# Hybrid decoder layer on one core: x transposed and w_in grouped by the host

## The chip, the cores and the metric

The kernel runs on one core of a Trainium2 chip. Its time is device microseconds of one execution, lower is better; several executions are timed and the median is given. Before the change the median of three is 529.26 us (526.42 to 530.28). One further execution was recorded by the hardware profiler; it took 522.21 us, and every row shown here comes from it.

The engines are TensorE (PE for matrix products, PEld for the loading of their stationary operand), VectorE (DVE), ScalarE (ACT), GpSimd (POOL) and SyncE (SP, which issues most transfers). Sixteen DMA engines move data between HBM and on-chip memory.

## What is computed

One decoder layer over 512 tokens of width 1024, in float32. Cut to what matters here:

```python
proj = x @ w_in                                   # (512,1024) @ (1024,2824)
ml_qk, ml_v, ml_o, ml_i, ml_f, a_q, a_k, a_v = jnp.split(proj, SPLIT_POINTS, axis=-1)
y = concat([mlstm_heads(...), sliding_window_attention(...)]) @ w_out
x = layer_norm(ALPHA * x + y)
x = layer_norm(ALPHA * x + hierarchical_moe(x))   # 32 experts, 4 groups, top 2 inside one group
```

The input projection is the first product of the layer. Everything else follows from it: the eight gate columns, the attention heads, the mLSTM heads, the output projection, the router, and at last 32 experts of 3 MB of weights each.

## The kernel before, in words

**The projection.** TensorE contracts over the partition axis, so x is needed with its 1024 features on partitions. The 512 tokens go in four chunks of 128 (`c` = 0 to 3). `xc[c]` receives a chunk as it lies in memory, tokens on partitions, 4 KB per token. `x_t(c)` transposes it with eight TensorE transposes of 128 by 128 into two PSUM banks, and then `split` writes each quarter (`q`, two blocks of 128 features) as a high part (`xh`, ScalarE, rounded to the fast float32 form) and a remainder (`xl`, VectorE, source minus high part).

**The weights.** `w_in` has 2824 columns and is taken in eleven groups of 264 or 256 columns, listed in `COLS`. `load_w(i)` fetches group `i` on SP's queue, the first group in three pieces (3, 3 and 2 blocks of 128 rows), the others in two pieces of four blocks. In memory a row of a group is one run of 1056 or 1024 bytes, and the next row is 11,296 bytes further on. `split_w(i)` splits each piece into `wh` and `wl` in the same way as x.

**The units.** `unit_att(i, c)` multiplies chunk `c` by one of the first three groups: 24 products, for each of the eight feature blocks high by high (line 244), low by high (line 245) and high by low (line 249). I call `unit_att(0, 0)` the first unit, `unit_att(0, 1)` the second, and so on; the fifth is `unit_att(1, 0)`. In the first unit all eight line-249 products come last, because the remainder `wl` is late. The next chunk's `x_t(c + 1)` is called inside a unit: before feature block 6 in the first unit, ahead of the second and third units otherwise. After these come the units for the mLSTM columns.

**The start.** SP issues in this order: `xc[0]`, the three pieces of group 0, `xc[1]` to `xc[3]`, then the pieces of group 1 and onward, as buffers come free. TensorE begins with `heat(WARM)`, products on zeros whose result nobody reads, then the transposes of chunk 0, then `heat(WARM2)`, then the first unit. The order on TensorE, VectorE and SP is the order of the code; ScalarE's is also in that opening part. GpSimd issues the small loads (biases, convolution weights, rotary tables) with its own queue, and later computes the rotary embedding (`rope`) for the attention heads, whose first input is the ScalarE copy `tq` of the fifth unit (line 271).

**After the projection.** Expert weights of the six static experts are fetched when the projection's loads are all issued; the others can only be fetched when the router has chosen the order. The x that the residual needs is loaded a second time, in its natural layout.

Of the kernel before, what the change touches and what calls it, by code (L numbers as in the profile page):

```python
# [22 lines left out]
DM = 1024  # L23
NCH = 4
P = 128
DIN = 2824
NE = 32
DE = 256
CAP = 64

ORDER = "BBBCABABABBCC"
NP = len(ORDER)
STATIC = 6
# [22 lines left out]
def place():  # L56

    na, nb = ORDER.count("A"), ORDER[STATIC // 2:].count("B")
    first = iter(range(STATIC))
    a, b = iter(range(STATIC, STATIC + na)), iter(range(STATIC + na, STATIC + na + 2 * nb))  # L60
    c = iter(range(STATIC + na + 2 * nb, NE))
    seats, base, cap = [], [0] * NE, [0] * NE
    for p, kind in enumerate(ORDER):
        src = {"A": (a, c), "B": (b, b), "C": (c, c, c, c)}[kind] if p >= STATIC // 2 else (first, first)
# [9 lines left out]
def ap_of(src, offset, dims):  # L74
    return bass.AP(tensor=src.tensor, offset=src.offset + offset, ap=dims)
# [1 line left out]

@with_exitstack
def layer_kernel(ctx, tc, x, w_in, conv_w, conv_b, gate_bias, norm_w, sinks, w_out, ln1_w, ln1_b,
                 w_gr, b_gr, w_er, b_er, w_gate, w_up, w_down, ln2_w, ln2_b, cos_t, sin_t, seat_t, out,  # L80
                 dbg=None):
    nc = tc.nc
    V, A, G, TE, SP = nc.vector, nc.scalar, nc.gpsimd, nc.tensor, nc.sync
# [36 lines left out]
    def bank(name, n=512, tag="m"):  # L120
        return PS.tile([P, n], F32, tag=tag, name=name, bufs={"m": 4, "t": 2, "pj": 2}[tag])
# [4 lines left out]

    x2 = x.rearrange("b s d -> (b s) d")
    o2 = out.rearrange("b s d -> (b s) d")
    win = w_in[0]
    xd = DR.tile([T, DM], F32, name="xd")  # L130

    yd = DR.tile([KEPT * P, DM], F32, name="yd")


    COLS = [(2048, 264), (2312, 256), (2568, 256)] + [(256 * i, 256) for i in range(8)]
    raws = {}

    THIRDS, HALVES = ((0, 3), (3, 3), (6, 2)), ((0, 4), (4, 4))
# [1 line left out]
    def wslot(name, i, m, dt=F32):  # L140
        t = slot(name, dt, "wr" if i else "ring0")
        return t[:, :m * COLS[i][1]].rearrange("p (j n) -> p j n", j=m)


    def wpair(i, m):
        if i:
            return [wslot(t, i, m, F32R) for t in ("wh", "wl")]
        n = m * COLS[0][1]
        t = slot("wh", F32R, "ring0")
        return [t[:, k * n:(k + 1) * n].rearrange("p (j n) -> p j n", j=m) for k in range(2)]  # L150

    def load_w(i):
        c0, n = COLS[i]
        raws[i] = []
        for j, m in THIRDS if i == 0 else HALVES:
            t = wslot("wraw", i, m)
            SP.dma_start(t, ap_of(win, j * P * DIN + c0, [[DIN, P], [P * DIN, m], [1, n]]))
            raws[i].append(t)

    xc = []  # L160
    for c in range(NCH):
        t = slot("xc")[:, :DM]
        SP.dma_start(t, x2[c * P:(c + 1) * P])
        xc.append(t)
        if c == 0:
            load_w(0)

    ident = C.tile([P, P], F32, name="ident")
# [19 lines left out]
    def split(hi, lo, src, eng=V):  # L188
        A.activation(hi, src, AF.Copy)  # L189
        eng.tensor_tensor(lo, src, hi, op=OP.subtract)  # L190
# [22 lines left out]
    xh = [slot("xh", F32R, "xt").rearrange("p (j n) -> p j n", j=2) for _ in range(4)]  # L213
    xl = [slot("xl", F32R, "xt").rearrange("p (j n) -> p j n", j=2) for _ in range(4)]

    def x_t(c):
        for g in range(2):
            p_ = bank("xt").rearrange("p (j n) -> p j n", j=4)
            for j in range(4):
                k = g * 4 + j  # L220
                TE.transpose(p_[:, j], xc[c][:, k * P:(k + 1) * P], ident)
            for h in range(2):
                q = g * 2 + h
                split(xh[q][:, :, c * P:(c + 1) * P], xl[q][:, :, c * P:(c + 1) * P],
                      p_[:, 2 * h:2 * h + 2])
                yield


    ws = {}
# [31 lines left out]
    def unit_att(i, c, late=False, mid=None):  # L261
        n = COLS[i][1]
        off = [0, 264, 520][i]
# [392 lines left out]
    with tc.manual_schedule(engines={ENG.PE, ENG.DVE, ENG.Activation}):  # L656
        warm = W.tile([P, P], F32, name="trif", bufs=1)
        V.memset(warm, 0.0)
        p_ = bank("warm")
# [449 lines left out]
    def pass_gu(xs, b, p, mid=None, parts=()):  # L1109
        pg = bank("pg")  # L1110
        for i in range(4):
            if i == 3 and mid:
                mid()
            if i and len(parts) >= i:
                parts[i - 1]()
            gu_part(pg, xs, b, pairs[p], TILES[ORDER[p]], i)
        return pg
# [25 lines left out]
    def pass_dn(ht, p):  # L1143
        return dn_mm(ht, pairs[p], TILES[ORDER[p]])

# [48 lines left out]
    q = C.tile([P, 5, 8], F32, name="slq")  # L1194
# [195 lines left out]
    with tc.manual_schedule(engines=MAN):  # L1390
# [108 lines left out]
        pgs = [bank("pg")]  # L1499
        gu_part(pgs[0], xs, 0, pairs[0], TILES[ORDER[0]], 0)  # L1500
        px = slots_b1()
# [11 lines left out]
    with tc.manual_schedule(engines={ENG.PE}):  # L1513
# [3 lines left out]
        h = pair_h(pgs[0])  # L1517
# [3 lines left out]
        h = pair_h(pgs[1])  # L1521
# [71 lines left out]
    with tc.manual_schedule(engines={ENG.PE, ENG.DVE}):  # L1593
        for p in range(2, NP - 1):
# [6 lines left out]
            h = pair_h(pg)  # L1601
# [66 lines left out]
    p = NP - 1  # L1668
    release(p - 1, True)
    prefetch(99)  # L1670
    with tc.manual_schedule(engines=MAN):
# [41 lines left out]
        h = pair_h(pg)  # L1713
# [44 lines left out]
    with tc.For_i(0, nmore, 1):  # L1758
# [20 lines left out]
_INS = ["x", "w_in", "conv_w", "conv_b", "mlstm_gate_bias", "mlstm_norm_w", "attn_sinks", "w_out",  # L1779
        "ln1_w", "ln1_b", "w_group_router", "b_group_router", "w_expert_router", "b_expert_router",  # L1780
        "w_exp_gate", "w_exp_up", "w_exp_down", "ln2_w", "ln2_b"]
# [8 lines left out]
            np.ascontiguousarray(np.concatenate([-s, s], 1)))  # L1790


def extra_inputs():
    _, base, cap = place()
    t = np.zeros((NE, 98), np.float32)
    t[:, 0:32], t[:, 32:64] = base, cap
    e = np.arange(NE)
    t[:, 96] = np.where(e < STATIC, 2000 * (STATIC - e), 0) + (NE - 1 - e) / 64
    t[:, 64:96] = t[:, 96]
    t[:, 97] = e  # L1800
    return list(zip(("rope_cos", "rope_sin", "seat_tab"), rope_tables() + (t,)))
# [19 lines left out]
```

## Time and profile before

| | us |
|---|---|
| median of three timed runs | 529.26 (526.42 to 530.28) |
| the profiled execution, whole | 522.21 |
| its span, first to last instruction | 520.5 |
| PE busy in the span | 475.8 (91%) |
| PEld, DVE, ACT, POOL busy | 324.1, 284.3, 161.2, 156.3 |
| line 221, the transposes of x, 32 products | 5.1 busy |

All positions in time are microseconds from the start of the span. A group of rows gives an engine's busy time, and the brackets at the end of a row say how long the engine stood idle before it and what ended that idle time. Adjacent instructions of one kind are merged into one row with a count. A product is pipelined, so the durations of neighbouring products overlap; the pace of a series is read from the starts. The profiled execution lies 7 us under the median of the timed runs.

### The profile page before, as it was taken

To read this page: it belongs to the slowest core of one execution; us is meant where nothing else is said; L and a number is where in the kernel's file an instruction comes from. 1 tells how busy PE (TensorE), PEld (TensorE's weight loads), DVE (VectorE), ACT (ScalarE), POOL (GpSimd) and SP (SyncE) were. 2 spreads that over 40 slices of the span, in tenths; PEclk is the share of its full clock that TensorE was granted. 3 is DMA by queue.
4 is the path that set the end of the run, shared out by engine and by line. 5 is a ranking of instruction groups with operands and counts; after the bars stand their busy time and mean duration, and the time that the engine had idled before them with its cause. 6 is when DMAs were issued, how large, how long until landed. Compare 5 with 4: busy or idle time off the path is not lost. (4 is left out here: it accounts for less than half of the span.)

```text
span 520.5 us, 8320 instructions
## 1 busy us (share of the span) xinstructions
PE 475.8 (91%) x2992; PEld 324.1 (62%) x2992; DVE 284.3 (55%) x635; ACT 161.2 (31%) x349; POOL 156.3 (30%) x178
## 2 busy tenths in 40 slices
PE   6999899999999999979799999999799949999881
PEld 6999678879899987758654736272263533353320
DVE  3543697984278685597876303012032036776953
ACT  3552565786444231333320202111021101131310
POOL 5579904323120100655650000000002334300431
PEclk9999999999999999999789999999899979998996
DMA  8724212220983548195929999999999999999740
GB/s 222 227 82 127 77 42 81 82 81 25 346 318 82 169 156 230 66 345 170 375 83 351 399 341 393 393 411 422 412 421 414 418 415 413 423 420 421 319 162 21
DMA packets 44605, 134.71 MB, mean 259 GB/s; under 512 B 6734, under 2 KB 18014, under 8 KB 41232
## 3 DMA queue, kind: packets, MB, share of 16 engines
q1 hardware_dynamic: 41504, 126.04, 64.7%
q0 software_dynamic: 3056, 8.10, 4.3%
q8 instruction: 24, 0.39, 0.3%
q14 instruction: 21, 0.17, 0.1%
HBM read 127.11 MB, written 8.91 MB: 261 GB/s over the span
## 5 line engine op out<-in xcount | busy, mean ns | idle before, releaser
L1106 PE MATMUL pg<-we,xs 128*32 128x512 f32 (+1 forms) x608 | 99.9, 601 | 3.3 <-DMA we<-in_w_exp_up 3.3
L1106 PEld LDWEIGHTS pg<-we,xs 128*32 128x32 f32 (+1 forms) x608 | 27.7, 120 | 60.6 <-issue 56.0
L244 PE MATMUL pj<-wh,xh 128*128 128x256 f32 (+1 forms) x224 | 63.3, 285 | 0.9 <-ACT wh L189 0.9
L245 PE MATMUL pj<-wh,xl 128*128 128x256 f32 (+1 forms) x224 | 62.3, 281 | 0.0
L1019 PE MATMUL xp<-ohr,x1h 128*128 128x256 f32 x192 | 51.3, 304 | 10.0 <-DVE xs L1025 8.2
L249 PE MATMUL pj<-wl,xh 128*128 128x256 f32 x192 | 52.5, 280 | 0.0
L1139 PE MATMUL yo<-we,ht 128*32 128x512 f32 (+1 forms) x304 | 50.0, 609 | 0.5 <-DVE ht L1131 0.5
L1019 PE MATMUL xp<-ohr,x1l 128*128 128x256 f32 x192 | 49.9, 297 | 0.0
L1019 PEld LDWEIGHTS xp<-ohr,x1h 128*128 128x128 f32 x192 | 39.4, 205 | 15.1 <-DVE xs L1025 8.4
L1157 POOL DMA_DIRECT2D yd<-y x8 | 4.4, 552 | 128.5 <-ACT y L1156 128.5
L244 PEld LDWEIGHTS pj<-wh,xh 128*128 128x128 f32 x224 | 42.1, 188 | 1.2 <-ACT wh L189 1.1
L245 PEld LDWEIGHTS pj<-wh,xl 128*128 128x128 f32 x224 | 42.1, 188 | 0.0
L1019 PEld LDWEIGHTS xp<-ohr,x1l 128*128 128x128 f32 x192 | 39.4, 205 | 0.0
L1131 DVE COPY ht<-ph 128x256 f32<-128x256 f32 x13 | 5.5, 423 | 57.1 <-PE ph L1129 57.1
L1121 ACT ACTIVATE hid<-pg 128x256 f32<-128x256 f32 x13 | 5.0, 383 | 101.8 <-PE pg L1106 101.8
L249 PEld LDWEIGHTS pj<-wl,xh 128*128 128x128 f32 x192 | 35.6, 188 | 0.0
L190 DVE TENSOR_TENSOR wl<-wraw,wh 128x1024 fp32r<-128x1024 f32 x14 | 21.5, 1552 | 22.7 <-ACT wh L189 14.4
L1139 PEld LDWEIGHTS yo<-we,ht 128*32 128x32 f32 (+1 forms) x304 | 14.2, 121 | 27.8 <-issue 25.8
L189 ACT ACTIVATE wh<-wraw 128x1024 fp32r<-128x1024 f32 (+2 forms) x23 | 23.2, 1021 | 11.8 <-PE pj L194 3.4
L193 PE MATMUL pj<-xh,wh 128*128 128x512 f32 x64 | 25.7, 402 | 0.0
L195 PE MATMUL pj<-xl,wh 128*128 128x512 f32 x64 | 25.5, 399 | 0.0
L1191 DVE TENSOR_TENSOR x<-x,cb 128x512 f32<-128x512 f32 x32 | 20.6, 680 | 9.0 <-PE cb L1190 8.9
(357 smaller groups left out, 964.3 us busy)
## 6 DMA issues: line engine op xcount, KB each, us to landing
we<-in_w_exp_gate SPq DMA_DIRECT2D x64, 512.0 KB, 12.4
we<-in_w_exp_up SPq DMA_DIRECT2D x64, 512.0 KB, 12.2
we<-in_w_exp_down SPq DMA_DIRECT2D x26, 1024.0 KB, 12.9
wraw<-in_w_in SPq DMA_DIRECT2D x20, 512.0 KB, 3.4
we<-in_w_exp_down SPq DMA_DIRECT2D x12, 512.0 KB, 10.3
yd<-y POOLq DMA_DIRECT2D x8, 512.0 KB, 7.9
xc<-in_x SPq DMA_DIRECT2D x4, 512.0 KB, 9.3
wo<-in_w_out SPq DMA_DIRECT2D x8, 256.0 KB, 4.3
```

Source lines behind the costliest of these rows:

```text
L189: A.activation(hi, src, AF.Copy)
L190: eng.tensor_tensor(lo, src, hi, op=OP.subtract)
L193: TE.matmul(o, lh, rh, start=start, stop=False)
L195: TE.matmul(o, lh, rl, start=False, stop=stop)
L244: TE.matmul(o, xh[j // 2][:, j % 2, cs], ws[i][j][0], start=j == 0, stop=False)
L245: TE.matmul(o, xl[j // 2][:, j % 2, cs], ws[i][j][0], start=False, stop=False)
L249: TE.matmul(o, xh[k // 2][:, k % 2, cs], ws[i][k][1], start=False, stop=k == 7)
L1019: TE.matmul(p_[:, j2, 0:P * n], w[c][:, 2 * g + j2], o[:, c, 0:P * n], start=c == 0 and s == 0 and j2 == 0, stop=c == NCH - 1 and s == 1 a ...
L1106: TE.matmul(pg[s:s + n], xs[k // 4][:, k % 4, P * b + s:P * b + s + n], ws[e][k // 4][:, :, k % 4], start=k == 0, stop=k == 7)
L1131: V.tensor_copy(ht, ph)
L1139: TE.matmul(py[u][s:s + n], ht[:, j, s:s + n], wt[e][2][j][:, 512 * u:512 * u + 512], start=j == 0, stop=j == 1)
L1191: V.tensor_add(x1[c][:, us], x1[c][:, us], b)
```

## The change

The host hands over two arrays in another layout. `w_in` is stored group by group, and inside a group partition by partition, so that all that one partition receives from one piece is a single run. x is stored a second time, as `x_columns`: four chunks, each with features on partitions. The natural x stays, for the residual. On the chip `x_t` has no transpose left: `split` reads `xc[c]` directly.

```diff
     def load_w(i):
-        c0, n = COLS[i]
+        n = COLS[i][1]
+        off = DM * sum(m for _, m in COLS[:i])
...
-            SP.dma_start(t, ap_of(win, j * P * DIN + c0, [[DIN, P], [P * DIN, m], [1, n]]))
+            SP.dma_start(t, ap_of(w_in, off + j * n, [[8 * n, P], [n, m], [1, n]]))
...
-        SP.dma_start(t, x2[c * P:(c + 1) * P])
+        SP.dma_start(t, x_tr[c])
...
     def x_t(c):
-        for g in range(2):
-            p_ = bank("xt").rearrange("p (j n) -> p j n", j=4)
-            for j in range(4):
-                k = g * 4 + j
-                TE.transpose(p_[:, j], xc[c][:, k * P:(k + 1) * P], ident)
-            for h in range(2):
-                q = g * 2 + h
-                split(xh[q][:, :, c * P:(c + 1) * P], xl[q][:, :, c * P:(c + 1) * P],
-                      p_[:, 2 * h:2 * h + 2])
-                yield
+        v = xc[c].rearrange("p (k n) -> p k n", k=8)
+        for q in range(4):
+            split(xh[q][:, :, c * P:(c + 1) * P], xl[q][:, :, c * P:(c + 1) * P], v[:, 2 * q:2 * q + 2])
+            yield
...
+def by_groups(w):
+    v = np.asarray(w).reshape(DM // P, P, DIN)
+    return np.concatenate([v[:, :, c:c + n].transpose(1, 0, 2).ravel() for c, n in COLS])
...
+def by_columns(x):
+    return np.ascontiguousarray(np.asarray(x).reshape(NCH, P, DM // P, P).transpose(0, 3, 2, 1)).reshape(NCH, P, DM)
```

On SP, at the start of the program, the issues stand in the same order, and the shape of the weight loads shows the runs: three blocks of 264 columns per partition before, and one run of 792 (3168 bytes) after; of the later groups four blocks of 256 before, and one run of 1024 (4096 bytes) after. Before:

```order
L163 DMA xc<-in_x 128x1024
L157 DMA wraw<-in_w_in 128x3x264 x2
L157 DMA wraw<-in_w_in 128x2x264
L163 DMA xc<-in_x 128x1024 x3
L157 DMA wraw<-in_w_in 128x4x256 x20
```

and of the change:

```order
L164 DMA xc<-in_x_columns 128x1024
L158 DMA wraw<-in_w_in 128x792 x2
L158 DMA wraw<-in_w_in 128x528
L164 DMA xc<-in_x_columns 128x1024 x3
L158 DMA wraw<-in_w_in 128x1024 x20
```

The loads of x keep their size and run length; only those of the weights have fewer and longer runs.

On ScalarE, in the same stretch, the high parts of x stand between those of the weights (`wh<-wraw`). Before, with what each row waits for:

```order
L189 ACTIVATE xh<-xt 128x2x128 [waits PE_49]
L189 ACTIVATE wh<-wraw 128x792 [waits DMAHW2_49]
L189 ACTIVATE xh<-xt 128x2x128 [waits DVE_49]
L189 ACTIVATE wh<-wraw 128x528 [waits DMAHW3_49]
L189 ACTIVATE xh<-xt 128x2x128 [waits PE_49]
L189 ACTIVATE xh<-xt 128x2x128 [waits DVE_49]
L189 ACTIVATE xh<-xt 128x2x128 [waits PE_49]
L189 ACTIVATE xh<-xt 128x2x128 [waits DVE_49]
L269 COPY tq<-pj 128x256 [waits DVE_49]
```

and of the change:

```order
L190 ACTIVATE wh<-wraw 128x792 [waits DMAHW2_49]
L190 ACTIVATE xh<-xc 128x2x128
L190 ACTIVATE wh<-wraw 128x528 [waits DMAHW3_49]
L190 ACTIVATE xh<-xc 128x2x128 [waits DMAHW4_49]
L190 ACTIVATE xh<-xc 128x2x128 x3
L264 COPY tq<-pj 128x256 [waits DVE_49]
```

The places are the same; the four high parts of a chunk now wait once, for the chunk's load, where they waited in turn for TensorE's transposes and for VectorE's read of the same PSUM bank.

On TensorE, the first unit and the start of the second. Before:

```order
L245 MATMUL pj<-wh,xl 128x264
L221 MATMUL xt<-ident,xc 128x128 [waits DMAHW4_49]
L221 MATMUL xt<-ident,xc 128x128 x3
L221 MATMUL xt<-ident,xc 128x128 [waits PE_49]
L221 MATMUL xt<-ident,xc 128x128 x3
L244 MATMUL pj<-wh,xh 128x264 [waits Activation_49]
L245 MATMUL pj<-wh,xl 128x264 [waits DVE_49]
```

and of the change:

```order
L240 MATMUL pj<-wh,xl 128x264
L239 MATMUL pj<-wh,xh 128x264 [waits Activation_49]
L240 MATMUL pj<-wh,xl 128x264 [waits DVE_49]
L239 MATMUL pj<-wh,xh 128x264
L240 MATMUL pj<-wh,xl 128x264
L244 MATMUL pj<-wh,xh 128x264 x6
L244 MATMUL pj<-wh,xh 128x264 [waits DVE_49]
```

The wait for the load of chunk 1 (DMAHW4) stood inside the first unit, ahead of its last two feature blocks; it is gone from TensorE, and chunk 1 is waited for by ScalarE and VectorE alone. The other three groups of eight transposes are gone in the same way, and the ten products on zeros stand in one row at the start. Apart from these rows the orders on TensorE, VectorE and ScalarE are the same to the end of the program; on GpSimd a few constant fills of the first microseconds change places.

## Rows read from the trace of the kernel before

**Rows 1.** The page: busy tenths in forty slices of 13 us.

```profile
PE   6999899999999999979799999999799949999881
...
DMA  8724212220983548195929999999999999999740
```

**Rows 2.** Busy us (x instructions) by engine, then granted clock, DMA share, GB/s.

```profile
22.00:260.00 238.00, 226.40 (x1461) 197.56 (x1461) 164.81 (x376) 111.15 (x258) 96.28 (x94) 0.98 0.46 156
...
280.00:490.00 210.00, 194.83 (x1229) 93.86 (x1226) 77.82 (x161) 31.35 (x55) 29.00 (x33) 0.97 1.01 407
```

**Rows 3.** Timeline of TensorE, 0 to 26 us: start, us, what, idle before.

```profile
1.10 2.93 PE L663 MATMUL warm<-trif 128*128 128x128 f32 x12 [1.10 <-DVE mcol L444]
4.23 1.94 PE L221 MATMUL xt<-ident,xc 128*128 128x128 f32 x8 [0.20 <-DMA xc<-in_x]
...
12.17 1.09 PE L221 MATMUL xt<-ident,xc 128*128 128x128 f32 x8 [1.97 <-DMA xc<-in_x]
...
15.37 0.37 PE L244 MATMUL pj<-wh,xh 128*128 128x264 f32 x1
...
18.37 1.04 PE L221 MATMUL xt<-ident,xc 128*128 128x128 f32 x8
19.16 0.37 PE L244 MATMUL pj<-wh,xh 128*128 128x264 f32 x1
...
25.11 0.28 PE L244 MATMUL pj<-wh,xh 128*128 128x256 f32 x1
```

**Rows 4.** Timeline of ScalarE, 9 to 29 us.

```profile
9.33 0.64 ACT L189 ACTIVATE wh<-wraw 128x528 fp32r<-128x528 f32 x1
12.87 0.38 ACT L189 ACTIVATE xh<-xt 128x256 fp32r<-128x256 f32 x1 [2.90 <-PE xt L221]
...
22.84 2.01 ACT L189 ACTIVATE wh<-wraw 128x1024 fp32r<-128x1024 f32 x2
...
28.33 0.35 ACT L271 COPY tq<-pj 128x256 f32<-128x256 f32 x1
```

**Rows 5.** VectorE: a remainder in the timeline; the later ones, ns min/median/max.

```profile
10.43 0.70 DVE L190 TENSOR_TENSOR wh<-wraw,wh 128x528 fp32r<-128x528 f32 x1
...
L190 DVE TENSOR_TENSOR wl<-wraw,wh x14: 1217/1480/2323, 23.9 to 144.1; 128x1024 fp32r<-128x1024 f32 x14
```

**Rows 6.** Issue of chunk 1; two loads, KB and us from issue to landing.

```profile
2.78 0.47 SPq L163 DMA_DIRECT2D xc<-in_x  x1
...
xc<-in_x SPq DMA_DIRECT2D x1, 512.0 KB, 9.3
...
wraw<-in_w_in SPq DMA_DIRECT2D x1, 264.0 KB, 6.8
```

**Rows 7.** The table by stretches of Rows 2, of short stretches.

```profile
0.00:10.00 10.00, 7.80 (x40) 7.32 (x40) 3.05 (x7) 4.63 (x8) 4.91 (x13) 1.00 0.81 214
...
8.00:9.00 1.00, 0.31 (x3) 0.10 (x1) 0.16 (x1) 0.70 (x1) 0.00 (x0) 1.00 1.08 398
...
10.00:11.00 1.00, 0.20 (x2) 0.00 (x0) 1.00 (x3) 0.00 (x0) 0.00 (x0) 1.00 1.09 144
11.00:12.00 1.00, 0.00 (x0) 0.00 (x0) 0.13 (x1) 0.00 (x0) 0.84 (x1) 1.00 0.90 218
...
30.00:35.00 5.00, 5.00 (x45) 5.00 (x44) 2.86 (x2) 1.34 (x3) 4.92 (x5) 1.00 0.51 150
...
140.00:145.00 5.00, 5.00 (x45) 5.00 (x45) 0.88 (x1) 3.03 (x5) 2.78 (x2) 1.00 1.02 417
```

**Rows 8.** GpSimd's transfers from 10 to 11 us: packets, MB, share.

```profile
q0 software_dynamic: 37, 0.00, 11.0%
```

**Rows 9.** GpSimd: the cosine table's issue, its landing, the first rotary operation.

```profile
17.84 0.81 POOL L695 DMA_DIRECT2D csn<-in_rope_cos  x1
...
csn<-in_rope_cos POOLq DMA_DIRECT2D x1, 128.0 KB, 4.8
...
28.77 1.32 POOL L340 TENSOR_TENSOR rope<-tq,csn 128x512 f32<-128x512 f32 x1 [8.80 <-ACT tq L271]
```

More of the change, by code (lines that the diff above doesn't have):

```diff
@@ L29 @@
 CAP = 64
+COLS = [(2048, 264), (2312, 256), (2568, 256)] + [(256 * i, 256) for i in range(8)]
 ORDER = "BBBCABABABBCC"
@@ L79, in layer_kernel @@
 def layer_kernel(ctx, tc, x, w_in, conv_w, conv_b, gate_bias, norm_w, sinks, w_out, ln1_w, ln1_b,
-                 w_gr, b_gr, w_er, b_er, w_gate, w_up, w_down, ln2_w, ln2_b, cos_t, sin_t, seat_t, out,
+                 w_gr, b_gr, w_er, b_er, w_gate, w_up, w_down, ln2_w, ln2_b, cos_t, sin_t, seat_t, x_tr, out,
                  dbg=None):
@@ L128, in layer_kernel @@
     o2 = out.rearrange("b s d -> (b s) d")
-    win = w_in[0]
     xd = DR.tile([T, DM], F32, name="xd")
     yd = DR.tile([KEPT * P, DM], F32, name="yd")
-    COLS = [(2048, 264), (2312, 256), (2568, 256)] + [(256 * i, 256) for i in range(8)]
     raws = {}
@@ L1809 @@
     arrays, args = {}, []
-    named = [(n, np.ascontiguousarray(inputs[n])) for n in _INS]
-    named += extra_inputs()
+    named = [(n, np.ascontiguousarray(by_groups(inputs[n]) if n == "w_in" else inputs[n])) for n in _INS]
+    named += extra_inputs() + [("x_columns", by_columns(inputs["x"]))]
     for name, a in named:
```

## The prediction

> **What bounds the kernel now.** I read the forty slices first [rows 1]: TensorE is near full nearly everywhere, and the DMA engines are full in slice 1 and again from slice 22 to 37, with long thin stretches between. So there are three parts. The table by stage [rows 2] says which engine sets each: from 22 to 260 us TensorE is busy 226 of 238 us while the DMA share is 0.46, and from 280 to 490 us the DMA engines are full (share 1.01, 407 GB/s) because the expert weights pass. Neither part starts by a clock of its own: the middle one hangs on the projection's first products, and the last one cannot fetch its chosen experts before the router. What is won at the start should therefore shift all the rest.
>
> The start is read from TensorE's timeline [rows 3]. The reader is to see three things there: eight transposes before the first unit; a hole of 1.97 us inside the first unit, until the load of chunk 1 has landed at 12.1 us (issue 2.78 plus 9.3 [rows 6]); and two more groups of eight transposes, one just before the second unit's start at 15.37, one of 0.79 us between the second unit and the third (18.37 to 19.16). From 12.17 on TensorE has no idle bracket as far as these rows go. The second unit's start and the transposes behind it are what can move.
>
> **The change part by part.** I work out when the second unit could start, and compare. The reference is 15.37 + 0.79 = 16.16, since the transposes at 18.37 go as well; the next units follow without a gap up to the fifth at 25.11 [rows 3].
>
> *Transposes.* All 32 go. The first eight (1.94 us [rows 3]) lie beside the wait for the first weights: price nothing; without them ScalarE still waits for those weights. The other 24 were on the path, and are in the comparison.
>
> *Splits from the loaded chunk.* The source of `xh` and `xl` is now SBUF, not PSUM. ScalarE from PSUM takes 0.38 for 256 columns; from SBUF 0.64 for 528 and 2.01 for twice 1024 [rows 4], a slope of 0.75 ns a column, so 0.44 for 256. VectorE from SBUF takes 0.70 for 528 and at least 1.217 for 1024 [rows 5], so 0.42 for 256; the same rows reach 2.323, so up to 0.8 when it is disturbed. Four of these take at most 3.2 us, and a unit takes 2.9 to 3.0 (15.37 to 18.37), so from the third unit on they stay hidden beside the unit before. In the second they show at its head: first product 0.44 after the load, the next 0.42 later, which equals an unbroken start about 0.7 us after the load.
>
> *Longer runs.* What does a load of 1 KB runs cost? From 30 to 35 us only projection weights pass, at 150 GB/s for a share of 0.51, which is 294 GB/s if the engines were full; with the expert weights' long runs it is 417 at 1.02, or 409 [rows 7]. Group 0 has 1024 rows of 1056 bytes, 1.08 MB: 3.68 us at 294, 2.64 at 409. That is 1.0 us saved ahead of chunk 1. The Trainium skill, "DMA: Bandwidth & Descriptors", section "Specifications", puts the smallest transfer for line rate at 512 bytes. By it a run of 1056 bytes would already go at full rate, this saving would be nothing, and chunk 1 would land as late as before; this case's rows, 294 against 409, disagree, and it remains a rival below.
>
> *What 1.0 us is worth for chunk 1.* At least 1.0: landing at 11.1. At most more, because the stretch from 10 to 12 us is slow: 144 and 218 GB/s against 398 at 8 to 9 us, though the engines are full [rows 7]. Beside them GpSimd's queue has packets that carry next to nothing, 37 of them in a microsecond [rows 8]; these are its element loads of the convolution weights, which the change leaves alone. By 10.0 us 2.14 MB have moved, by 12.0 us 2.50 MB, when chunk 1 is nearly landed. With 1.0 us more at 0.37 MB/us the 2.50 MB are reached at 10.0. So chunk 1 lands between 10.0 and 11.1; I take the middle, 10.6, because neither the place of the slow stretch nor the lag of the last DMA engine is seen well enough to prefer an end.
>
> *The first unit.* Would it be ready? Its last remainder is 10.43 + 0.70 = 11.13 now [rows 5], on a third piece that landed 6.8 us after its issue [rows 6] and that ScalarE rounded at 9.33 [rows 4]. Part of the 1.0 us saved is taken back by the splits queued ahead, so I put the remainder at 10.5 and the end of the last two products at 10.8. The second unit waits for the later of 10.8 and 10.6 + 0.7 = 11.3.
>
> *Sum.* 16.16 - 11.3 = 4.9 us. With chunk 1 at 11.1 it is 4.4; at 10.0 the first unit binds and it is 5.4.
>
> *What must keep up.* The fifth unit needs group 1's high parts, which ScalarE began at 22.84 with no idle bracket [rows 4]; wanted 4.9 earlier, at 17.9. Its loads come 1.0 us earlier from group 0 and some 0.5 us a piece from their own 4 KB runs; if that cover were short, TensorE would wait the difference there. GpSimd's rotary work began at 28.77, released by the copy of the fifth unit's result [rows 4, 9], and would begin at 23.9; its cosine table lands at 17.84 + 4.8 = 22.6 [rows 9], so 1.3 us of cover are left, and a gain above 6 would be cut there. The weights of later groups are asked for when buffers come free, which moves with the compute; their faster landing is hidden under a TensorE without idle time, so I cost it at nothing.
>
> **The rivals.**
>
> *Only the transposes count.* The runs bring nothing for chunk 1: it lands at 12.1, second unit at 12.8, gain 16.16 - 12.8 = 3.4. For it: the skill's line on 512 bytes, and that chunk 1 is held by GpSimd's element loads. Against: the two rates above.
>
> *The opening loads run free.* Chunk 1, group 0 and chunk 0 are 2.13 MB; at 409 GB/s from 1.9 us on they are in at 7.1, the weights at 5.9, the first unit ends about 9.7 and the second follows: gain 6.5. Against: the slow stretch has its cause elsewhere.
>
> *Shifted, but given back.* Some step in the middle is held by something that does not move (a table's landing, a small load, the order on SP), or the DMA-full part eats the shift. Gain 0 to 1. Against: every release that I followed leads back to the fifth unit.
>
> *TensorE's clock, the slower side.* The opening transposes went at half pace: eight in 1.94 us against 1.04 for the same eight at 18.37 [rows 3]; those are the levels of 1.2 and 2.4 GHz, though the granted clock stands at 1.00 in the stretch [rows 7]. TensorE had been at work from 1.10 us on. Without the transposes its twenty warm-up instructions run in one series and end near 6.0 (twelve take 2.93 [rows 3]), and what follows is a first unit that stops for each of its three pieces of weights. If it is then still, or again, at the lower level while the first group's units run, each unit costs some 2.9 us more. That decides from 4.9 / 2.9 = 1.7 units: with three units after the first at the lower level the loss is 8.7, net 3.8 slower, 533. The Trainium skill, "TensorE: Matmul & The Clock Gate", Part 1, says that an idle TensorE falls back to the lower level and must be busy for a time to return, which is this danger in general. Against: the hole of 1.97 us did not lower it here (1.04 to 1.09 us per eight afterwards).
>
> That the runs are not joined is excluded by the loads' shapes, 792 columns in one.
>
> **How the numbers follow.** Forecast (4.9, bounds 4.4 to 5.4): chance 0.62. Only the transposes (3.4): 0.15. Free loads (6.5): 0.12. Given back: 0.06. Clock: 0.05. The sum stands against the profiled 522.2 us, which becomes 517.3. The timed median lies at 529.26, 7 us above it, and I subtract the same from that: **524.4 us**. The cases reach from 522.8 (free loads) to 525.9 (transposes only), and the median of three runs that spread from 526.4 to 530.3, with a profiled one at 522.2, is uncertain by some 2 us more: 520.0 to 528.0. One per cent, about what a measurement here can tell from no change, is 5.3 us; the forecast lies just under it. So a little under half of the forecast's chance (0.29), most of the free loads' (0.10) and little of the transposes' (0.02) give faster by over 1%: 0.41. The clock case gives slower, 0.05; the rest, 0.54, is within 1%.
>
> **What would show it.** In the changed profile the second unit should begin near 11.3 with no product between it and the first, the load of chunk 1 land 7.2 to 8.3 us after issue, the fifth unit begin near 20.2, the rotary work near 23.9, the full DMA part start and end some 5 us earlier. Chunk 1 at 9.3 us from issue means the runs brought nothing there. Products of the second unit starting 0.24 us apart, not 0.12, mean the clock. A fifth unit 5 us earlier with the rotary work or the end where they were means that the shift was given back; I would then be wrong on what follows the start, not on the start.

## The result, and the profile after

| timed together | the change, us | before, us | ratio, 95% interval |
|---|---|---|---|
| first | 523.75 (520.36 to 526.11, 15 runs) | 526.91 (15) | 0.9937 (0.9913 to 0.9960) |
| second | 521.23 (520.18 to 524.86, 6) | 528.16 (11) | 0.9897 (0.9847 to 0.9948) |
| third | 523.33 (518.97 to 524.98, 12) | 527.61 (35) | 0.9924 (0.9893 to 0.9956) |

All runs of the table together: 523.5 against 527.5 us, a gain of 4.0 us or 0.8%. Forecast were 524.4 us and a gain of 4.9. So the time came out; the reasons came out only in part, and that is what the rest is about. Some kernels below have single runs some 10 us above their others; ranges and medians include these, ratios leave them out.

The two first profiled executions can't be compared by their spans: that of the change took 525.79 us, near the top of its runs, that of before 522.21, below nearly all of its runs. What can be compared is the opening. TensorE after the change (start, us, what, idle before):

```profile
1.10 4.64 PE L658 MATMUL warm<-trif 128*128 128x128 f32 x20 [1.10 <-DVE mcol L439]
6.01 0.53 PE L239 MATMUL pj<-wh,xh 128*128 128x264 f32 x1 [0.28 <-ACT wh L190]
...
11.38 0.59 PE L239 MATMUL pj<-wh,xh 128*128 128x264 f32 x1 [3.62 <-ACT wh L190]
11.76 0.42 PE L240 MATMUL pj<-wh,xl 128*128 128x264 f32 x1
11.98 0.42 PE L239 MATMUL pj<-wh,xh 128*128 128x264 f32 x1
...
13.74 1.96 PE L244 MATMUL pj<-wh,xh 128*128 128x264 f32 x8
15.50 0.42 PE L239 MATMUL pj<-wh,xh 128*128 128x264 f32 x1
...
16.60 0.28 PE L244 MATMUL pj<-wh,xh 128*128 128x264 f32 x1
16.72 0.28 PE L239 MATMUL pj<-wh,xh 128*128 128x264 f32 x1
...
24.79 0.28 PE L239 MATMUL pj<-wh,xh 128*128 128x256 f32 x1
```

The transposes are gone, as the diff says. But TensorE stood still for 3.62 us, not for chunk 1 as in [rows 3], but for the second piece of group 0; then its products started 0.22 us apart up to 16.6, and only from there 0.12. The second unit began at 15.50, not at 11.3, and followed the last eight products of the first unit (from 13.74) without idle time. The fifth began at 24.79, where [rows 3] has 25.11. ScalarE, in the same stretch:

```profile
10.46 0.86 ACT L190 ACTIVATE wh<-wraw 128x792 fp32r<-128x792 f32 x1 [3.88 <-DMA wraw<-in_w_in]
...
13.08 1.34 ACT L190 ACTIVATE xh<-xc 128x256 fp32r<-128x256 f32 x4 [0.91 <-DMA xc<-in_x_columns]
...
28.01 0.35 ACT L266 COPY tq<-pj 128x256 f32<-128x256 f32 x1
```

Both loads are late. Chunk 1 landed at 12.1 in the profiled execution before [rows 6], and ScalarE rounded the second piece at 8.30 there:

```profile
8.30 0.86 ACT L189 ACTIVATE wh<-wraw 128x792 fp32r<-128x792 f32 x1 [1.27 <-DMA wraw<-in_w_in]
```

After the change chunk 1 took 10.4 us from its issue at 2.67, not 9.3:

```profile
DMA to landing us min/median/max: 10.4/10.4/10.4
```

The table by short stretches (busy us of PE, PEld, DVE, ACT, POOL, then granted clock, DMA share, GB/s) answers to [rows 7]:

```profile
8.00:9.00 1.00, 0.00 (x0) 0.00 (x0) 0.00 (x0) 0.00 (x0) 0.00 (x0) 1.00 0.98 365
9.00:10.00 1.00, 0.00 (x0) 0.00 (x0) 0.00 (x0) 0.00 (x0) 0.00 (x0) 0.88 1.06 289
10.00:11.00 1.00, 0.00 (x0) 0.00 (x0) 0.00 (x0) 0.54 (x1) 0.00 (x0) 0.50 1.05 234
11.00:12.00 1.00, 0.62 (x3) 0.62 (x4) 0.64 (x1) 1.00 (x3) 0.00 (x0) 0.50 1.05 244
...
14.00:15.00 1.00, 1.00 (x6) 1.00 (x6) 0.96 (x3) 0.42 (x2) 0.73 (x2) 0.50 1.02 410
...
30.00:35.00 5.00, 5.00 (x45) 5.00 (x44) 2.52 (x2) 1.35 (x4) 4.92 (x4) 1.00 0.50 170
```

Three things are to be seen. The slow stretch of the DMA engines, share over 1 at 230 to 290 GB/s, is still there. And the granted clock fell to 0.50, the level of 1.2 GHz, while TensorE stood still, and stayed there to 16.6 us. From 30 to 35 us, where the engines are half busy, the longer runs move 170 GB/s where [rows 7] has 150. GpSimd's rotary work, to set beside [rows 9], moved by the same 0.32 us as the fifth unit:

```profile
28.45 1.32 POOL L335 TENSOR_TENSOR rope<-tq,csn 128x512 f32<-128x512 f32 x1 [6.57 <-ACT tq L266]
```

### The profile page after: what moved, and what is told of

Same layout as the page of the kernel before. It is cut to its first block, busy times and chain, and to the rows that moved or that the text cites. A ratio compares the mean times of both kernels' runs of the same rounds, so it can differ in the third digit from the quotient of the medians.

```text
span 524.1 us, 8258 instructions
## 1 busy us (share of the span) xinstructions
PE 477.0 (91%) x2960; PEld 321.5 (61%) x2960; DVE 281.5 (54%) x635; ACT 161.2 (31%) x349; POOL 155.8 (30%) x178
## 5 line engine op out<-in xcount | busy, mean ns | idle before, releaser
L1101 PE MATMUL pg<-we,xs 128*32 128x512 f32 (+1 forms) x608 | 102.8, 605 | 8.3 <-DMA we<-in_w_exp_up 8.3
L239 PE MATMUL pj<-wh,xh 128*128 128x256 f32 (+1 forms) x224 | 64.4, 289 | 3.9 <-ACT wh L190 3.9
L240 PE MATMUL pj<-wh,xl 128*128 128x256 f32 (+1 forms) x224 | 63.5, 285 | 0.3 <-DVE xl L191 0.3
L1014 PE MATMUL xp<-ohr,x1h 128*128 128x256 f32 x192 | 50.0, 299 | 5.5 <-DVE xs L1020 3.0
L1014 PE MATMUL xp<-ohr,x1l 128*128 128x256 f32 x192 | 48.7, 292 | 0.0
L239 PEld LDWEIGHTS pj<-wh,xh 128*128 128x128 f32 x224 | 43.2, 193 | 4.5 <-ACT wh L190 4.4
L240 PEld LDWEIGHTS pj<-wh,xl 128*128 128x128 f32 x224 | 43.2, 193 | 0.6 <-DVE xl L191 0.6
L1014 PEld LDWEIGHTS xp<-ohr,x1l 128*128 128x128 f32 x192 | 38.3, 200 | 0.0
L191 DVE TENSOR_TENSOR wl<-wraw,wh 128x1024 fp32r<-128x1024 f32 x14 | 19.8, 1429 | 24.3 <-ACT wh L190 24.3
L194 PE MATMUL pj<-xh,wh 128*128 128x512 f32 x64 | 25.7, 402 | 0.0
L196 PE MATMUL pj<-xl,wh 128*128 128x512 f32 x64 | 25.5, 399 | 0.0
L199 POOL TENSOR_SCALAR lnmv<-lnmv 128x1 f32<-128x1 f32 x9 | 4.1, 451 | 72.1 <-DVE lnmv L1638 49.8
## 6 DMA issues: line engine op xcount, KB each, us to landing
xc<-in_x_columns SPq DMA_DIRECT2D x4, 512.0 KB, 10.4
```

Source lines behind the costliest of these rows:

```text
L194: TE.matmul(o, lh, rh, start=start, stop=False)
L196: TE.matmul(o, lh, rl, start=False, stop=stop)
L239: TE.matmul(o, xh[j // 2][:, j % 2, cs], ws[i][j][0], start=j == 0, stop=False)
L240: TE.matmul(o, xl[j // 2][:, j % 2, cs], ws[i][j][0], start=False, stop=False)
L1014: TE.matmul(p_[:, j2, 0:P * n], w[c][:, 2 * g + j2], o[:, c, 0:P * n], start=c == 0 and s == 0 and j2 == 0, stop=c == NCH - 1 and s == 1 a ...
L1101: TE.matmul(pg[s:s + n], xs[k // 4][:, k % 4, P * b + s:P * b + s + n], ws[e][k // 4][:, :, k % 4], start=k == 0, stop=k == 7)
```

## The experiments

Since one execution can mislead, each kernel below was profiled and timed, and both kernels were profiled three times. The table collects what the timelines show, in us: when the second piece of group 0 is rounded, when chunk 1 is first used, the starts of the fifth unit, of the rotary work and of the first layer norm's scaling on ScalarE, and the span; and the granted clock from 10 to 15 us.

| kernel | piece 2 | chunk 1 | unit 5 | rotary | norm | span | clock |
|---|---|---|---|---|---|---|---|
| before | 8.30 | 12.17 | 25.11 | 28.77 | 209.6 | 520.5 | 1.00 |
| before, second | 8.64 | 12.04 | 24.99 | 28.65 | 211.1 | 522.1 | 1.00 |
| before, third | 8.85 | 12.68 | 28.38 | 32.04 | 214.5 | 529.0 | 0.68 |
| w_in alone (e2) | 8.52 | 11.77 | 24.71 | 28.37 | 210.8 | 523.4 | 1.00 |
| before, late small loads (e6) | 7.25 | 9.62 | 23.07 | 27.16 | 206.6 | 520.4 | 1.00 |
| after | 10.46 | 13.08 | 24.79 | 28.45 | 209.3 | 524.1 | 0.50 |
| after, second | 10.15 | 13.04 | 24.16 | 27.82 | 210.3 | 523.1 | 0.50 |
| after, third | 8.51 | 11.70 | 22.03 | 25.68 | 208.2 | 520.3 | 0.72 |
| after, 1 KB runs (e10) | 8.46 | 12.32 | 23.02 | 26.69 | 207.4 | 518.6 | 0.50 |
| x alone (e1) | 8.30 | 12.03 | 22.03 | 25.70 | 208.0 | 519.5 | 0.66 |
| after, heat (e4) | 9.30 | 12.07 | 21.80 | 25.46 | 207.8 | 520.3 | 1.00 |
| after, late small loads (e3) | 7.90 | 9.88 | 22.57 | 26.83 | 206.8 | 518.9 | 0.51 |
| x alone, late small loads (e7) | 7.12 | 9.44 | 20.23 | 25.82 | 209.0 | 521.1 | 1.00 |
| the same, heat (e8) | 6.68 | 8.81 | 22.63 | 27.01 | 206.5 | 518.0 | 0.90 |

### Which half of the change gains: e1, e2, e10

e1 keeps the new x and loads w_in in its natural layout; e2 keeps the new w_in and transposes x on the chip as before; e10 has both, but with each group's rows in runs of 1 KB.

```diff
# e1, from the change
-            SP.dma_start(t, ap_of(w_in, off + j * n, [[8 * n, P], [n, m], [1, n]]))
+            SP.dma_start(t, ap_of(w_in, j * P * DIN + c0, [[DIN, P], [P * DIN, m], [1, n]]))
# e2, from the change: x_t with its transposes, and
-        SP.dma_start(t, x_tr[c])
+        SP.dma_start(t, x2[c * P:(c + 1) * P])
# e10, from the change
-            SP.dma_start(t, ap_of(w_in, off + j * n, [[8 * n, P], [n, m], [1, n]]))
+            SP.dma_start(t, ap_of(w_in, off + j * P * n, [[n, P], [P * n, m], [1, n]]))
...
-    return np.concatenate([v[:, :, c:c + n].transpose(1, 0, 2).ravel() for c, n in COLS])
+    return np.concatenate([v[:, :, c:c + n].ravel() for c, n in COLS])
```

Expected of e1: 

> x comes transposed from the host, w_in stays in its natural layout with runs of 1056 and 1024 bytes. If the longer runs bring chunk 1 earlier (my prediction's term of 1.0 us), this gains less than the whole change: 16.16 - 12.8 = 3.4 us by the prediction's own sum, against its 4.9. Rival, from the profile of the changed kernel, where the second piece of group 0 landed at 10.4 us against 8.3 before: the long runs themselves make the first pieces late; then this kernel gains at least as much as the whole change (3.2 us or more), its second piece is rounded near 8.3 us, and the fifth unit starts near 21.7 instead of 24.8.

Expected of e2: 

> w_in comes grouped from the host, x is transposed on the chip as before. By the prediction chunk 1 lands 1.0 to 2.1 us earlier and the time falls by as much, 1 to 2 us. By the rival (long runs delay the second piece, here from 8.3 to some 10.4 us) nothing is gained or 1 to 2 us are lost, since the hole in front of chunk 1's transposes moves in front of the fourth feature block.

Expected of e10: 

> The changed kernel with w_in's groups laid out dense but in runs of one row (1 KB), as long as those of the natural layout; x as changed. If the length of the runs matters, the DMA engines move less in 5 to 15 us than in the changed kernel and the median is 1 us or more above it. If the runs don't matter (theory now: GpSimd's small loads set the landing times and the transposes are the gain), pieces and chunks land as with x alone (second piece 8.3 to 9.5, chunk 1 near 12), the granted clock holds better than in the changed kernel, and the time is that of x alone, 522 us.

Measured: e1 522.08 us (519.6 to 524.84), ratio 0.9887 (0.9854 to 0.9921); e2 525.79 us (521.72 to 531.85), ratio 0.9963 (0.9930 to 0.9995), both against 528.33. e10 took 522.26 us (519.52 to 525.55), ratio 0.9924 (0.9893 to 0.9955), beside 523.33 for the change on the same chip. So x is the gain; the grouped w_in alone is worth some 2.5 us by the medians (0.3 to 3.7 by the interval), and nothing that can be seen once x has changed. The long runs do not bring chunk 1 forward: 11.77 with them alone, 12.03 without. Of e10's expectation the landings and the time came; that the granted clock holds better did not (0.50). e1 also showed every sign of its rival, that the long runs make the second piece late; the repeats below return to that.

### Is the lower clock a cost, and whose: e4

```diff
             if mid and mid[0] == j:
                 par(mid[1])
+            if mid and mid[0] == 6 and j == 3:
+                heat(10)
```

Ten products on zeros, two instructions each, go between the first and the second piece of group 0; their result is not read.

Expected: 

> The changed kernel with ten more products on zeros in the first unit, between the first and the second piece of weights, where TensorE stood idle for 3.6 us. Theory of the clock: in the changed kernel's profile the granted clock is 0.50 from 9.8 to 16.6 us, and some 24 products went at 0.22 us instead of 0.12, about 2.3 us; with TensorE kept busy the clock stays at 1.00, and 1.5 to 2.3 us are won over the changed kernel. Rival: the products behind the wait were waiting for splits and loads anyway, or the timed runs have no such long wait; then the time stays within 0.5 us of the changed kernel.

Measured: 523.25 us (521.98 to 525.46), ratio 0.9911 (0.9884 to 0.9939). The profile of e4 shows the clock at 1.00 from 5 to 15 us and the eight late products of the first unit 1.13 us long, not 1.96:

```profile
7.81 2.29 PE L660 MATMUL warm<-trif 128*128 128x128 f32 x19
10.21 0.39 PE L241 MATMUL pj<-wh,xh 128*128 128x264 f32 x1
...
12.03 1.13 PE L246 MATMUL pj<-wh,xh 128*128 128x264 f32 x8
13.01 0.28 PE L241 MATMUL pj<-wh,xh 128*128 128x264 f32 x1
...
21.80 0.28 PE L241 MATMUL pj<-wh,xh 128*128 128x256 f32 x1
```

With chunk 1 rounded from 12.07, the fifth unit starts 9.73 us later. That distance, from chunk 1 to the fifth unit, is a fair measure where chunk 1 lands near the end of the first unit (chunk 1 counts from its first transpose or its first rounding): 12.94 in the kernel before, 12.95 in its second execution, 12.94 in e2; 9.73 in e4, and 10.00 to 11.71 in e1, e10 and the three executions of the change, all of which spent part of it at the lower level. So the transposes were worth 3.2 us, and up to 2.0 of it were taken back. Most of that is the lower level: from the first product on the second piece to the second unit the three executions of the change took 4.12, 4.13 and 3.81 us, e4 2.80. In the kernel before the lower level cost 2.8 us where it came: 15.70 from chunk 1 to the fifth unit in its third execution. In e3, e7 and e8 chunk 1 lands early and waits for the first unit, in e6 TensorE waits for chunk 2 as well, so that their distances, 10.8 to 13.8, say nothing of this. The time of e4 is nevertheless not shown to be better than that of the change: 523.25 lies between its medians, and the 1.5 to 2.3 us that were expected of it are not seen.

### What holds the loads up: e3, e6

GpSimd's small loads (rotary tables, norm weight, sinks, convolution weights, router biases) are held back by one copy from chunk 3, and SP loads the gate bias. GpSimd's constant fills move ahead of that copy.

```diff
+    SP.dma_start(gbias, ap_of(gate_bias, 0, [[0, P], [1, 8]]))     # e3: behind chunk 3; e6: behind chunk 1
...
+        G.tensor_copy(csn[:, 0:1], xc[3][:, 0:1])                  # then all small loads of GpSimd
+        G.dma_start(cosd, cos_t.rearrange("(c p) d -> p c d", p=P))
```

e3 does this to the change:

> The changed kernel, with GpSimd's small loads (rotary tables, norm weights, sinks, convolution weights and biases) held until chunk 3 of x has landed, and the gate bias loaded on SP's queue after chunk 3. Theory: these element loads are what starves the DMA engines at 4 to 7 us and at 9 to 12 us, so without them the second piece is rounded by 7.5 us, chunk 1 lands by 9, and the time falls by 2.5 to 4 us below the changed kernel. Rival: the holes are the HBM's or SP's own (SP's issue of chunk 3 took 2.2 us); then the landings stay within 0.5 us and the time does not move.

e6 does it to the kernel before, whose layout and transposes it keeps:

> The kernel before, with GpSimd's small loads (rope tables, norm weight, sinks, convolution weights, router biases) held until chunk 3 has landed and the gate bias loaded by SyncE right behind chunk 1. Theory: the small loads starve the big ones in the opening. Then chunk 1 lands near 10 us instead of 12.0, the DMA engines move over 330 GB/s in 5 to 10 us instead of 241, the fifth unit starts 2 us sooner (near 23) and the kernel takes about 2 us less, 526 us. Rival: the run lengths limit the loads; natural w_in keeps its 1 KB runs here, so 5 to 10 us stays near 250 GB/s, chunk 1 near 12 and the time at 528.

Measured: e3 521.44 us, but six runs from 514.46 to 532.02, and its ratio of 0.9757 (0.9718 to 0.9796) rests on three of them: too few to say what it gains. e6 521.67 us (517.31 to 523.29), ratio 0.9890 (0.9835 to 0.9945): without any new layout as much as the change. The loads are no longer held; e6, 10 to 12 us, beside 144 and 218 GB/s in [rows 7], and the transposes of its chunk 1 on TensorE:

```profile
5.00:10.00 5.00, 4.57 (x30) 4.36 (x29) 3.73 (x7) 3.47 (x7) 1.97 (x5) 1.00 0.89 302
10.00:12.00 2.00, 2.00 (x19) 1.96 (x17) 1.00 (x4) 1.04 (x3) 1.74 (x8) 1.00 1.00 396
14.00:15.00 1.00, 1.00 (x10) 1.00 (x9) 0.51 (x2) 0.51 (x3) 0.71 (x1) 1.00 1.08 383
...
9.62 1.10 PE L223 MATMUL xt<-ident,xc 128*128 128x128 f32 x8 [0.43 <-DMA xc<-in_x]
```

At the same share of 1.0 the engines move 396 GB/s from 10 to 12 us, where they moved about 180 beside GpSimd's element loads, and from 14 to 15 us 383 with runs of 1 KB alone. Chunk 1 is there at 9.62, behind weights in 1 KB runs. The slow stretch of the kernel before had no such runs in it at all, as its transfers from 10 to 12 us show:

```profile
DMA packets 151, 0.36 MB, mean 181 GB/s; under 512 B 64, under 2 KB 64, under 8 KB 151
```

64 packets are under 512 bytes, none between that and 2 KB, and the other 87 can only be the 4 KB rows of x. So it was the small loads, not the length of the runs, that set when chunk 1 lands; which of the small loads, this edit does not separate. Two expectations of e6 failed: from 5 to 10 us it moves 302 GB/s, not over 330, and the time fell by 6.5 us, not 2. The fifth unit did come some 2 us earlier (23.07); where the rest lies, its one profiled execution (span 520.4) does not show.

### Both together: e7, e8

e7 is e1 with the small loads held as in e6; e8 is e7 with the ten products of e4.

> x laid out by the host, w_in in its natural order, and GpSimd's small loads held as in the run before. Theory of the small loads: chunk 1 lands near 10 us, the second unit starts near 11 us or, with TensorE at the lower clock level behind its wait, near 13; the fifth unit starts near 20.5 and the kernel takes about 520 us, 1.5 us less than with x alone (522.1). Rival (run lengths): chunk 1 near 12, fifth unit near 22, 522 us. Third: the rope tables now land later than the fifth unit's scaling, rope starts no sooner than 25.7 and the time is 522 us though chunk 1 lands early.

> As the run before, with ten products that add zero between the first and the second piece of group 0, so that TensorE doesn't stand still there. If the lower clock level in the opening costs what its rows say (products at 0.22 instead of 0.12 us), the granted clock is 1.00 from 5 to 15 us, the fifth unit starts 1.5 to 3 us sooner than in the run before (18 to 19) and the kernel takes 518 to 519 us. If the clock costs nothing there (TensorE waits for loads anyway), fifth unit and time are those of the run before.

Measured: e7 522.70 us (517.73 to 524.58), ratio 0.9895 (0.9835 to 0.9955); e8 521.67 us (518.44 to 533.41), ratio 0.9880 (0.9815 to 0.9945). e7's fifth unit starts at 20.23, which is the 20.2 that I had predicted for the change, and the kernel is no faster for it than with x alone. Of the three expectations the third came by its numbers, rotary work no sooner than 25.7 and 522 us. The profile shows where the rest went. The timeline of VectorE in e7, the remainders of the weights:

```profile
24.80 5.74 DVE L192 TENSOR_TENSOR wl<-wraw,wh 128x1024 fp32r<-128x1024 f32 x2 [3.09 <-ACT wh L191]
```

That of GpSimd beside it:

```profile
24.31 1.55 POOL L719 TENSOR_SCALAR csa<-csa 128x512 f32<-128x512 f32 x1
25.82 2.23 POOL L336 TENSOR_TENSOR rope<-tq,csn 128x512 f32<-128x512 f32 x1
```

And that of ScalarE, which waits for the next group's two halves:

```profile
30.42 1.06 ACT L191 ACTIVATE wh<-wraw 128x1024 fp32r<-128x1024 f32 x1 [1.21 <-DMA wraw<-in_w_in]
35.16 1.06 ACT L191 ACTIVATE wh<-wraw 128x1024 fp32r<-128x1024 f32 x1 [3.68 <-DMA wraw<-in_w_in]
```

Two remainders took 5.74 us beside GpSimd's work, where two take 3.17 in e1 and e6; the longest single one took 3.70, the shortest of that stretch of the program 1.22. GpSimd's first rotary product took 2.23 beside them, 1.32 in [rows 9]. The buffer came free late, SP asked for the next half group at 30.56, it landed at 35.1, and TensorE stood still (the timelines of SP and TensorE):

```profile
30.56 0.37 SPq L157 DMA_DIRECT2D wraw<-in_w_in  x1
...
36.53 0.38 PE L240 MATMUL pj<-wh,xh 128*128 128x256 f32 x1 [2.14 <-ACT tq L267]
```

The first layer norm was at 209.0, 1.0 us behind e1, which had started its fifth unit 1.8 us later. The Trainium skill, "Trainium Architecture — The Big Picture", section "What this means for kernel authors", says that VectorE and GpSimd share one port pair to SBUF, and that it locks out rather than divides; the rows agree that each slows the other, and show no more than that.

My own edit is part of it: the held loads keep GpSimd issuing until 24.3 (e7) and 25.5 (e8), and the rotary work then waits for GpSimd itself, not for the tables. In e8 the ten products also stood in the way: there the second piece came at 6.68, so that they were no longer hidden in a hole; they ran from 7.93 to 11.56, 3.6 us where e4 took 2.5, and the fifth unit started at 22.63, not at 18 to 19. That expectation failed.

### The two kernels again: e5, e9, e11, e12

> The changed kernel once more, beside the three that follow. If its late pieces are its own (the long runs keep the 16 DMA engines further apart while GpSimd's small loads are under way), the second piece of group 0 is rounded after 9.0 us again, chunk 1 after 11.8, and the fifth unit starts between 22 and 25. If they were one unlucky execution, the second piece is rounded near 8.3 us, chunk 1 near 10.6 as predicted, TensorE's granted clock stays at 1.00 before 15 us and the fifth unit starts near 20. Median 523.5 us by both.

> The kernel before, once more, for a second profiled execution of it: the first took 522.21 us, some 5 us less than the median of its other runs (526.9), so it may not show what the typical one pays. Theory A (the difference lies in the opening): the second piece of group 0 or chunk 1 lands later than the 8.3 and 12.0 us of the first one, rope starts after 29.5 us instead of 28.77, and the whole middle moves with it. Theory B (it lies behind the projection): rope again at 28.8 and the first layer norm at 209.6 us, and the stretch from there to the end takes 313 to 316 us instead of 310.9, as it did in the profiled executions of the changed kernel (314.8 and 312.9). Ratio 1.00.

> The kernel before, a third profiled execution, to see how far one execution stands from another: the two theories as for the second one, and a ratio of 1.00.

> The changed kernel, a third profiled execution, on the same chip as the two of the kernel before. The first two had the second piece at 10.46 and 10.15 us, chunk 1 at 13.06 and 13.04 and rope at 28.45 and 27.82 us. If these are the kernel's own, the third has the same within 0.7 us, and the gain that the median shows (3.3 and 6.9 us so far) is to be found behind the projection or in openings of the kernel before that are later than the one profiled; if they were chance, rope starts near 24 to 26 us.

Measured: e5 and e12 are the second and third row of the first table. e9 took 526.93 us, ratio 0.9998 (0.9967 to 1.0029), e11 528.22 us, ratio 1.0021 (0.9991 to 1.0051): the kernel before against itself, as it should be. The second piece of the change was late again in e5 (10.15), but not in e12 (8.51). But whether the long runs make it late more often is open. With them and the small loads in place it was rounded at 8.51 to 10.46 (five executions: the change, e2, e4), with 1 KB runs at 8.30 to 8.85 (five: before, e1, e10); with the small loads held, at 7.90 (e3) against 6.68 to 7.25. And the opening of the kernel before is no constant either. In e11 chunk 1 came 0.5 us later than in the first execution, TensorE had stood still for 1.58 and for 1.92 us, and this time the clock fell (TensorE, then the table):

```profile
9.77 0.39 PE L244 MATMUL pj<-wh,xh 128*128 128x264 f32 x1 [1.58 <-ACT wh L189]
...
12.68 1.97 PE L221 MATMUL xt<-ident,xc 128*128 128x128 f32 x8 [1.92 <-DMA xc<-in_x]
...
10.00:15.00 5.00, 3.08 (x17) 2.88 (x17) 2.10 (x4) 1.32 (x4) 3.28 (x9) 0.68 1.02 304
15.00:20.00 5.00, 5.00 (x30) 5.00 (x29) 2.30 (x7) 2.16 (x7) 4.61 (x15) 0.64 1.11 303
```

Its rotary work started at 32.04, 3.3 us behind the first. Theory A (the opening) holds for these 3.3 of the 8.5 us that its span is longer; 1.6 lie between the rotary work and the first layer norm, and 3.6 behind that, where theory B puts them. e9 shows neither: its rotary work started at 28.65, and its last part took 311.1 us. From the first layer norm to the end the three executions before took 310.9, 311.1 and 314.5 us, those of the change 314.8, 312.9 and 312.1. The change gains nothing there, and both scatter by some 3 us.

## Why the prediction was right, and where it was wrong

**All the rest shifts with the opening: right.** From the rotary work to the first layer norm the distance is 180.8 us before and 180.8 after; over the six executions of the two kernels it lies between 180.8 and 182.5. There is no wait in between that gave the shift back. It holds up to a gain of some 3 us: e7 was 4.9 us ahead of the first execution before at the fifth unit, and 0.6 ahead at the first layer norm.

**The transposes and the splits: right.** The rival that counted the transposes alone priced them at 3.4 us; e4 against before and e2 shows 3.2. The splits from SBUF took 0.40 to 0.42 us on ScalarE and 0.42 to 0.52 on VectorE, where the sum has 0.44 and 0.42. Its bound of 0.8 each, 3.2 for four, would not have fitted beside a unit of 3.0, as it says; it did not come to that.

**Longer runs, 1.0 us: the step that failed.** I took 294 GB/s for 1 KB runs from a stretch in which the DMA engines were half busy [rows 7], and scaled it to a full one. Where they are full and no element loads pass, the natural layout moves 383 GB/s (e6, 14 to 15 us) and the grouped one 410 (after, the same stretch). In that stretch runs of 1 KB gave 380 to 386 in all eight executions of before, e1, e6, e7, e8 and e10, and the longer ones 410 to 426 in the five of the change, e2 and e4; only e3, with long runs and none of GpSimd's packets in that stretch, has 336, and no run shows why. 1.08 MB then differ by 2.82 - 2.63 = 0.2 us. Rate over share in the half-busy stretch, 294 before and 340 after (170 at 0.50), is neither of these rates, so it can't be scaled to 1; what the packets spend their time on there, no run shows. The Trainium skill, "DMA: Bandwidth & Descriptors", section "Specifications", puts full rate at 512 bytes and up; 383 against 410 stands nearer to that than my 294 against 409 did.

**What 1.0 us is worth for chunk 1: wrong with it.** Landing was to be at 10.0 to 11.1, and was at 13.1, 13.0 and 11.7 by ScalarE's first use. I had seen GpSimd's element loads there [rows 8], and still let the slow stretch be passed by starting earlier. It wasn't: only e3 and e6 to e8, which move those loads away, land chunk 1 before 10. By [rows 8] the small packets themselves take 11% of the engines' time, so it is not their own time that is missing; the large packets take longer beside them. By an estimate from the transfers, 99 packets of the hardware queue that took 92.3% of 16 engines' time from 10 to 12 us before took 0.30 us each, and 114 that took 101.6% from 14 to 15 us after 0.14 us. The Trainium skill, "DMA: Bandwidth & Descriptors", section "Queues, rings and completion order", says that each engine takes turns between the queues packet by packet. That the two queues disturb each other agrees with e6 against before; why by half, no run here shows. And chunk 1 was not even what held the second unit: in all three executions of the change it followed the first unit without idle time. The term of 10.8 us for the first unit was the one that bound, and it was mis-sized: with the second piece at 10.46 and the lower pace it became 15.50 in the first execution.

**The clock, the slower rival: the mechanism came, the size did not.** It had a chance of 0.05 at 8.7 us. The lower level came in all three executions of the change, and cost 0.6 to 2.0 us of the 3.2 (11.71, 11.12 and 10.33 from chunk 1 to the fifth unit, against 9.73; a late second piece may have a small part in it), one unit's products at most and not three units', because the clock came back while the products ran. It fell as well in e1, e3 and e10, which also lack the opening transposes and the added products (in e7 the pace was the lower one too, though the column reads 1.00), and of the five executions with the transposes (before, e2, e6) in one, e11. What I had used against it, that the hole of 1.97 us [rows 3] had not lowered it, was one execution; in e11 a hole of 1.92 us, 1.0 us of products behind another of 1.58, did. The Trainium skill, "TensorE: Matmul & The Clock Gate", Part 1, had named that danger; the rows of the change and of e11 agree with it. What spared the first execution before, no run here shows. In the change the 4.2 us from 11.3 to 15.50 are 1.3 by the lower pace (4.12 against 2.80 in e4 from the second piece's first product to the second unit); the other 2.9 are the late second piece. Chunk 1 alone, at 13.1 and 0.7 us of splits, would have let the second unit start at 13.8.

**The number.** 3.2 us for the transposes, less 0.6 to 2.0 for the clock, would be 1.2 to 2.6 us. The mean of three openings is 2.5 us earlier (fifth unit 23.66 against 26.16), 1.4 if e11, whose clock fell, is left out. The mean of the three spans is 1.4 us shorter (522.5 against 523.9). The timed gain is 4.0. The difference of 1.5 us from the openings, and of 2.6 from the spans, is not placed: three profiled executions of each, whose spans differ among themselves by 3.8 and 8.5 us, can't carry it. That the typical execution before is more often like e11 would explain it, but wasn't shown. So 524.4 came from a gain of 4.9 in which 1.5 us, 1.0 from the runs and 0.5 from what follows them, did not exist, and it was taken from 529.26, where 61 runs have 527.5. That the two errors leave it 0.9 us from the measured 523.5 is luck.

## What to carry to other kernels

Before pricing a faster load, look at what else the DMA engines carry in that stretch: a share of 1.0 at half the usual rate is a reason to see which queues have packets there. Moving GpSimd's small loads out of the opening gave as much here (e6, 0.989) as laying out x on the host, and the two did not add up; in e7's profile the next chain (weights' buffers, VectorE beside GpSimd, GpSimd's own late issues) took the rest back. And when a change takes work away from TensorE just where it waits for data, look at the granted clock: what the work had cost, it may have paid for by keeping the clock up.

## What the runs showed of the hardware

**The clock falls in some executions and not in others, at the same place.** Between 65 and 73 us some executions lose 1.5 us. TensorE of the kernel before, first execution:

```profile
65.62 0.55 PE L382 MATMUL sc<-kT,qs 128*128 128x128 f32 x3 [2.29 <-DVE qs L364]
...
67.53 0.40 PE L194 MATMUL pj<-xh,wl 128*128 128x512 f32 x1
67.77 0.40 PE L195 MATMUL pj<-xl,wh 128*128 128x512 f32 x1
```

and the second:

```profile
65.55 0.55 PE L382 MATMUL sc<-kT,qs 128*128 128x128 f32 x3 [2.29 <-DVE qs L364]
...
67.47 0.63 PE L194 MATMUL pj<-xh,wl 128*128 128x512 f32 x1
67.89 0.63 PE L195 MATMUL pj<-xl,wh 128*128 128x512 f32 x1
```

The same wait of 2.29 us, the same products; once they start 0.24 us apart, once 0.42. It is in the executions of the change too: from the rotary work to the first layer norm they all take 180.8 or some 182.4 us, and nothing between.

**The granted clock is not the whole pace.** In e7 the products from 6.9 to 10.4 us start 0.22 us apart, while the clock is shown as 1.00:

```profile
9.08 0.42 PE L240 MATMUL pj<-wh,xh 128*128 128x264 f32 x1
9.30 0.42 PE L241 MATMUL pj<-wh,xl 128*128 128x264 f32 x1
```

```profile
5.00:10.00 5.00, 4.44 (x19) 3.85 (x19) 3.95 (x8) 3.74 (x8) 3.75 (x8) 1.00 0.93 310
```

The opening transposes [rows 3] were such a case too. Where products don't wait, their starts tell the level better than the column.
